# A split-float32 attention layer on one core: a longer distance from scores to transposes and values, four sized probability buffers, and a weight split moved between engines

## The chip, the cores and the metric

One core of a Trainium2 chip runs the whole program. The metric is the device time of one execution in microseconds (us), median over runs. Engines are named as the profile names them: PE (TensorE matmuls and transposes), PEld (its weight loads), DVE (VectorE), ACT (ScalarE), POOL (GpSimd), SP (SyncE, which issues DMAs).

## The reference

One layer with multi-head latent attention in float32: S = 1024 tokens, model width 1024, 16 heads, chunks of 64.

```python
u = h @ w_in
c_q, c_kv, k_rope, z = jnp.split(u, [...])
q = (rmsnorm(c_q, q_norm) @ w_q_b).reshape(B, S, MLA_HEADS, MLA_NOPE + MLA_ROPE)
kv = (rmsnorm(c_kv, kv_norm) @ w_kv_b).reshape(B, S, MLA_HEADS, MLA_NOPE + MLA_V)
...
for blk in range(S // Q_BLOCK):          # query blocks of 128
    s = (q_nope . k_nope + q_rope . k_rope) * scale     # keys 0 .. q1
    s = jnp.where(k_chunk[None, :] <= q_chunk[:, None], s, -jnp.inf)
    prob = jax.nn.softmax(s, axis=-1)
    outs.append(prob @ v[:, :q1])
...
return (o * jax.nn.silu(z)) @ w_out
```

Behind it the layer adds a per-layer embedding, gated by a sigmoid of the residual stream.

## The kernel before

Every float32 product is made of three matmuls in a faster format: each operand is split into a high part (a rounded copy) and a low part (what is left of it, `sub_hi`, L91), and `pairs` runs high by high, high by low, low by high. So a matmul operand always costs a cast (often on ACT) and a subtraction (DVE or GpSimd).

The program has five stages, by time of the profiled execution: the projections of u (0 to 69 us), the z gate and the rotary part of the queries (69 to 188), attention (188 to 520), the output projection (520 to 630), the embedding gate (630 to 741).

In the second stage a loop over eight column blocks `c` (L500 to L528) multiplies h with the z weights (L510); for c from 2 to 5 `project_r` (L421) also multiplies the query latent with a piece of the rotary weights `w_r` (`product_q`, nine matmuls, L417, for each half). Its results are multiplied by cosine and sine on DVE (L429), split into `zT`/`rh` on ACT (L431) and lows on GpSimd, and written to memory by DMAs that GpSimd issues (L434). The rotary weights come through `load_split` (L391): a DMA into one of two staging tiles `ws`, a copy into `wrh` (L397) and a subtraction into `wrl` (L91), both on GpSimd. Each of `wrh` and `wrl` has one buffer. The per-head weights (`wq`, `wk`, `wv`) use the same function.

In attention a step is one pair of a head and a query block i, 128 steps in all. Block i has (i+1)*128 keys. ORDER = (7, 0, 6, 1, 5, 2, 4, 3) alternates large blocks (4 to 7, over 512 keys) with small ones. A step (loop at L690) issues `scores` of its block (L597: matmuls L608, mask L611, row maximum L613 on DVE, exp L618 on ACT with its row sum, which ACT reads out in a second instruction); then the projections that fall due (`project_k` L544, `project_v` L563, `project_q` L585, by the tables K_AT, V_AT, Q_AT of step numbers within a head); then `values` (L659, matmuls L667, output L671 on ACT and L672 on DVE) of a finished half head, LAGV steps later; then `prob_transposes` (L640) of the block LAG steps back: 128x128 transposes on PE (L118), up to four into one tile, a cast to the high part on ACT (L656), a subtraction on DVE (L91). The `p` tiles of halves are `pt0` and `pt1`.

Scores of a large block lie in `ps_big`, of which there are two (a tile of 1024 columns each); all else in attention (`ps_tr`, `ps_pj`, `ps_o`) shares four tiles of 512 columns. A `ps_big` tile is free again when the exp has read it. The exp writes into a probability tile, of which there are three of 1024 columns (`prob_tile`, L541). The framework puts each engine's instructions into a fixed order in advance and adds the waits; the source order and the buffers decide what it may do.

Of the kernel before, what the change touches and what calls it, by code (L numbers as in the profile page):

```python
# [9 lines left out]
F32 = mybir.dt.float32  # L10
# [7 lines left out]
P = 128  # L18
S = 1024
# [4 lines left out]
QL = 384  # L24
# [13 lines left out]
LAST = (7, 0, 6, 1, 5, 2, 3, 4)  # L38
WARM = 9
V_FIRST = (1, 1, 5, 3)  # L40
V_AT, K_AT, Q_AT, ROPE_AT = (5, 5, 3, 3), (1, 3), (7, 5), 4
LAG, LAGV, LEAD, ODD_AT = 2, 4, 2, 1
TWO_PI = 2.0 * math.pi


# [6 lines left out]
def mla_ple_kernel(ctx, tc, x, x_t, p_t, pos, norm_g, w_c, w_z, q_norm, w_q, w_r, kv_norm, w_k, w_v,  # L52
# [7 lines left out]
    V, A, G = nc.vector, nc.scalar, nc.gpsimd  # L60

    def pool(name, bufs=1, **kw):
        return tc.tile_pool(name=name, bufs=bufs, **kw)
# [3 lines left out]
    def ps_big():  # L67
        return psum.tile([P, 1024], F32, tag="big", name="ps_big", bufs=2)

    def ps_tr():  # L70
        return psum.tile([P, 512], F32, tag="one", name="ps_tr", bufs=4)
# [18 lines left out]
    def sub_hi(eng, lo, src, hi):  # L90
        eng.tensor_tensor(out=lo, in0=src, in1=hi.bitcast(F32), op=ALU.subtract)  # L91
# [295 lines left out]
    att1 = late.enter_context(pool("att1", side="right"))  # L387
    att2 = late.enter_context(pool("att2", side="right"))
    k_hi, k_lo = zip(*([att2.tile([P, S], F32R, name=f"k_{z}{e}") for z in ("hi", "lo")] for e in range(2)))

    def load_split(src, cols, name, bufs, home=att1):  # L391
        n = math.prod(cols)
        stg = att1.tile([P, 512], F32, tag="ws", name="ws", bufs=2)[:, :n]
        nc.sync.dma_start(out=stg, in_=src)
        hi = home.tile([P, n], F32R, tag=name + "h", name=name + "h", bufs=bufs)
        lo = home.tile([P, n], F32R, tag=name + "l", name=name + "l", bufs=bufs)
        G.tensor_copy(out=hi, in_=stg)  # L397
        sub_hi(G, lo, stg, hi)
        return tuple(z.rearrange("p (k n) -> p k n", k=cols[0]) for z in (hi, lo))

    wk_of, wv_of, wq_of, q_of, rq_of = {}, {}, {}, {}, {}
# [1 line left out]
    def weights(h):  # L403
        if h >= H:
            return
        if h % 2 == 0:
            wq_of[h // 2] = load_split(w_q[h // 2], (QL // P, P), "wq", 1)
            wk_of[h // 2] = load_split(w_k[h // 2], (KVL // P, P), "wk", 1)
        if h % 4 == 0:
            wv_of[h // 4] = load_split(w_v[h // 4], (KVL // P, 256), "wv", 1)  # L410
# [82 lines left out]
    zw = zph.enter_context(pool("zw", reuse_waits="tile"))  # L493
    cs = [zw.tile([P, S], F32, name=f"cs{e}") for e in range(2)]

    def weights_r(g):
        return load_split(w_r[g], (QL // P, P), "wr", 1, zw)


    for c in range(KT):  # L500
        ps = ps_big()
        for k in range(KT):
            if k % 4 == 0:
                n = 2 * c + k // 4
                wz = wz_of.pop(n)
                if n + 2 < 2 * KT:
                    wz_of[n + 2] = z_weights(n + 2)
            for a, b in pairs:
                for hf in range(2):
                    nc.tensor.matmul(ps[:, hf * 512:(hf + 1) * 512], wz[b][:, k % 4, :],  # L510
                                     (hT_hi, hT_lo)[a][:, k, hf * 512:(hf + 1) * 512],
                                     start=k == 0 and a + b == 0, stop=k == KT - 1 and a == 1)
        V.tensor_tensor(out=zT[:, c, :], in0=ps, in1=rbc, op=ALU.mult)
        A.activation(out=zT[:, c, :], in_=zT[:, c, :], func=AF.Silu)
        if c < 2:
            u_transposes(*pend.pop(0))
        if c == 0:
            rope_tables()
        if c == 1:
            rope_key()  # L520
            wr = weights_r(0)
        if 2 <= c < 6:
            project_r(c - 2, wr, 0, zT[:, 6, :], zT[:, 7, :].bitcast(F32R))
            project_r(c - 2, wr, 1, rt_tile("rt"), rh_tile("rh"))
            if c < 5:
                wr = weights_r(c - 1)
        if c == 6:
            weights(0)  # L528
# [5 lines left out]
    att = atts.enter_context(pool("att"))  # L534
# [3 lines left out]
    vals = att.tile([P, NT, 2, 4, VD], F32R, name="vals")  # L538
    kst = {}

    def prob_tile():  # L541
        return att.tile([P, S], F32, tag="prob", name="prob", bufs=3)

    def project_k(c, hf):  # L544
        w = wk_of[c]
# [48 lines left out]
    def order(h):  # L594
        return LAST if h == H - 1 else ORDER

    def scores(h, i):  # L597
        e = h % 2
        q = q_of[h]
        qs = slice(i * P, (i + 1) * P)  # L600
        n = (i + 1) * P
        off = P if n == 640 else 0
        spans = {128: [(0, 256)], 640: [(0, 384), (384, 640)]}.get(
            n, [(a, min(a + 512, n)) for a in range(0, n, 512)])
        ps = ps_big() if n > 512 else ps_tr()
        for s0, s1 in spans:
            for a, b in pairs:
                nc.tensor.matmul(ps[:, off + s0:off + s1], q[a][:, qs], (k_hi, k_lo)[b][e][:, s0:s1],  # L608
                                 start=a + b == 0, stop=a == 1)
        s = ps[:, off:off + n]  # L610
        V.memset(s[0:64, n - 64:], MASKED)  # L611
        mx = small.tile([P, 1], F32, tag="mx", name="mx")
        V.tensor_reduce(out=mx, in_=s, axis=AX.X, op=ALU.max, negate=True)  # L613
        pr = prob_tile()
        if e == 0 and i == order(h)[0]:
            sums[h // 2] = small.tile([P, 2 * NT], F32, tag="l", name="l", bufs=2)
        l = sums[h // 2][:, e * NT + i:e * NT + i + 1]
        A.activation(out=pr[:, :n], in_=s, func=AF.Exp, bias=mx, scale=1.0, accum_out=l)  # L618
        return pr
# [72 lines left out]
    for n in range(len(blocks) + LAGV):  # L692
        if n < len(blocks):
            h, i = blocks[n]
            at = n % NT
            probs[n] = scores(h, i)
            if h % 2 == 0 and at == ODD_AT:
                odd_k()
            for t in range(NT):
                if h % 4 == 0 and at == (V_AT if h else V_FIRST)[t // 2]:  # L700
                    project_v(h // 4, t)
            if h + 1 < H:
                if h % 2 and at in K_AT:
                    project_k((h + 1) // 2, K_AT.index(at))
                if h % 2 and at == ROPE_AT:
                    rope_q(h + 1)
                    rope_q(h + 2)
                if h % 2 and at in Q_AT:
                    project_q((h + 1) // 2, Q_AT.index(at))
                if h % 2 and at == max(Q_AT):  # L710
                    weights(h + 3)
        h, i = blocks[n - LAGV]
        g = i // 4
        if n >= LAGV and i == [z for z in order(h) if z // 4 == g][-1]:
            values(h, g)
            if h % 2 and i == order(h)[-1] and n < len(blocks):
                normalise(h // 2, lambda hf: att1.tile([P, 512], F32, tag="ws", name="rlb", bufs=2), G)
        if n >= LAG and n - LAG < len(blocks):
            prob_transposes(*blocks[n - LAG], probs.pop(n - LAG))
        if n == len(blocks) - LEAD:  # L720
            og0 = out_part(rh_tile("a0h"), rt_tile("a0l").bitcast(F32R), 0, slice(0, KT - 1), G.tensor_copy)
# [96 lines left out]
    for t in range(NT):  # L818
# [7 lines left out]
        for i, cols in enumerate(spans):  # L826
            n = cols.stop - cols.start
# [74 lines left out]
```

## Time and profile before

| what | value |
|---|---|
| time, median of 3 runs | 740.62 us (740.1 to 742.89) |
| the profiled execution, its own time | 742.71 us |
| its span in the trace | 740.9 us |
| PE busy | 712.6 us, 96% of the span |
| PEld busy | 599.2 us, 81% |
| DVE busy | 525.6 us, 71% |
| ACT busy | 401.2 us, 54% |
| POOL busy | 209.2 us, 28% |

The span is what the trace covers; the execution's own time is 1.8 us longer. PE and PEld overlap: the weights of one matmul load while the one ahead runs. "Busy" counts from the start of an instruction to its modelled end, so that successive matmuls overlap in the rows; the pace of PE is read from one start to the next. PEclk is the granted clock as a share of full speed.

### The profile page before, as it was taken

Reading aid. Unit: us, or ns where it says so; the run is one execution under the profiler, and the core shown is the slowest. Engines: PE = TensorE matmul, PEld = TensorE weight load, DVE = VectorE, ACT = ScalarE, POOL = GpSimd, SP = SyncE. Lnnn points to the kernel's source line nnn. Section 1 sums busy time; section 2 is a strip of 40 time slices with the busy share of each in tenths; the row PEclk is TensorE's granted clock in tenths of the full one; section 3 lists DMA queues with packets and bytes.
Section 4 is the critical chain, followed back from the end, with each engine's and each line's share of the span. In section 5 each row is a group of like instructions: output and inputs, shape, how many; then the busy total and the mean of one; then the engine's idle time right before and its main releaser. Section 6 shows DMA issues by size and latency. Waiting matters only on the chain.

```text
span 740.9 us, 11048 instructions
## 1 busy us (share of the span) xinstructions
PE 712.6 (96%) x3776; PEld 599.2 (81%) x3776; DVE 525.6 (71%) x1270; ACT 401.2 (54%) x921; POOL 209.2 (28%) x204
## 2 busy tenths in 40 slices
PE   8999999979999999999999999999999999999995
PEld 7999888858887778878888788877768887888885
DVE  6995456641887787888788887888555239788854
ACT  6752344331777676777777776776443135243322
POOL 0004316670223232323324232156136132000000
PEclk9999999989999999999999999999999999999998
DMA  8812524462311212101121211033384021110101
GB/s 310 286 56 68 132 77 176 164 216 76 85 44 29 76 30 75 39 27 56 30 75 44 76 29 47 13 115 85 116 297 128 0 86 28 37 43 36 58 28 58
DMA packets 27191, 63.90 MB, mean 86 GB/s; under 512 B 4600, under 2 KB 9088, under 8 KB 27136
## 3 DMA queue, kind: packets, MB, share of 16 engines
q1 hardware_dynamic: 23312, 52.05, 22.6%
q0 software_dynamic: 3536, 11.02, 4.4%
q8 instruction: 30, 0.49, 0.3%
q14 instruction: 25, 0.20, 0.1%
q10 hardware_dynamic: 288, 0.14, 0.1%
HBM read 50.01 MB, written 13.18 MB: 85 GB/s over the span
## 4 chain that ended last, share of the span: by engine, by line
PE 69%; DVE 11%; ACT 8%; issue 4%; DMA 3%; POOL 3%; SPq 0%; ACTq 0%; DVEq 0%; POOLq 0%
PE ps_big L757 17%; PE ps_big L510 9%; PE ps_o L667 9%; PE ps_tr L118 6%; PE ps_big L608 5%; PE ps_pj L417 4%; PE ps_big L212 3%; PE ps_pj L569 3%; PE ps_pj L550 3%; ACT prob L618 3%; DVE pt1l L91 3%; PE ps_pj L757 3%; PE ps_big L213 3%; PE ps_tr L608 2%; DVE mx L613 2%
## 5 line engine op out<-in xcount | busy, mean ns | idle before, releaser
L757 PE MATMUL ps_big<-w,aTh 128*128 128x512 f32 (+1 forms) x480 | 140.2, 392 | 1.8 <-ACT sg L833 1.8
L757 PEld LDWEIGHTS ps_big<-w,aTh 128*128 128x128 f32 x480 | 90.1, 189 | 22.2 <-ACT sg L833 2.2
L118 PE MATMUL ps_tr<-ident,prob 128*128 128x128 f32 x576 | 84.6, 275 | 6.0 <-ACT prob L618 3.3
L757 PE MATMUL ps_big<-w,aTl 128*128 128x512 f32 (+1 forms) x240 | 85.1, 392 | 0.6 <-POOL aTl L91 0.5
L118 PEld LDWEIGHTS ps_tr<-ident,prob 128*128 128x128 f32 x576 | 66.5, 140 | 20.6 <-ACT prob L618 10.2
L674 POOL TENSOR_TENSOR zT<-o,zT 64x512 f32<-64x512 f32 x28 | 36.0, 1287 | 141.2 <-DVE o L672 141.1
L91 DVE TENSOR_TENSOR pt1l<-ps_tr,pt1h 128x512 fp32r<-128x512 f32 (+1 forms) x144 | 72.7, 536 | 3.9 <-ACT pt1h L656 2.5
L656 ACT CAST pt1h<-ps_tr 128x512 fp32r<-128x512 f32 (+1 forms) x144 | 62.0, 470 | 24.2 <-PE ps_tr L118 12.0
L618 ACT ACTIVATE prob<-ps_big,mx 128x1024 f32<-128x1024 f32 (+1 forms) x64 | 61.3, 958 | 18.3 <-DVE mx L613 17.1
L613 DVE TENSOR_REDUCE mx<-ps_big 128x1 f32<-128x1024 f32 (+1 forms) x64 | 64.9, 1015 | 0.3
L358 DVE SCALAR_TENSOR_TENSOR zl<-zs,g_col,zh 128x128 fp32r<-128x128 f32 x56 | 31.3, 607 | 32.9 <-ACT zh L357 32.6
L757 PEld LDWEIGHTS ps_big<-w,aTl 128*128 128x128 f32 x240 | 45.3, 189 | 11.4 <-POOL aTl L91 1.5
L608 PE MATMUL ps_big<-k_hi,qh 128*128 128x512 f32 (+2 forms) x128 | 48.6, 380 | 0.0
L608 PE MATMUL ps_big<-k_hi,ql 128*128 128x512 f32 (+2 forms) x128 | 46.5, 363 | 0.0
L608 PE MATMUL ps_big<-k_lo,qh 128*128 128x512 f32 (+2 forms) x128 | 46.1, 360 | 0.0
L357 ACT ACTIVATE zh<-zs,g_col 128x128 fp32r<-128x128 f32 x56 | 18.3, 392 | 50.2 <-DMA zs<-in_w_z 47.2
L667 PE MATMUL ps_o<-pt1h,vals 128*128 128x512 f32 (+3 forms) x128 | 42.9, 361 | 1.5 <-DVE pt1l L91 1.0
L113 ACT ACTIVATE jk<-xs 128x512 bf16<-128x512 f32 (+2 forms) x25 | 18.7, 750 | 42.3 <-DVE xs L835 35.1
L667 PE MATMUL ps_o<-pt1l,vals 128*128 128x512 f32 (+3 forms) x128 | 41.6, 363 | 0.0
L672 DVE TENSOR_TENSOR o<-ps_o,o 64x512 f32<-64x512 f32 x32 | 22.0, 688 | 25.3 <-ACT o L671 25.2
L618 ACT ACTIVATE prob<-ps_tr,mx 128x128 f32<-128x128 f32 (+1 forms) x64 | 33.8, 529 | 5.5 <-DVE mx L613 5.3
L91 DVE TENSOR_TENSOR pt0l<-ps_tr,pt0h 128x128 fp32r<-128x128 f32 (+2 forms) x80 | 33.2, 416 | 4.5 <-ACT pt0h L656 2.9
(289 smaller groups left out, 1806.7 us busy)
## 6 DMA issues: line engine op xcount, KB each, us to landing
zT<-in_x SPq DMA_DIRECT2D x8, 512.0 KB, 4.5
rlb<-rl SPq DMA_DIRECT2D x32, 128.0 KB, 3.0
wst<-in_w_out SPq DMA_DIRECT2D x8, 512.0 KB, 4.1
xs<-in_x SPq DMA_DIRECT2D x8, 512.0 KB, 7.0
wst<-in_ple_gate SPq DMA_DIRECT2D x8, 512.0 KB, 3.7
zs<-in_w_z SPq DMA_DIRECT2D x14, 256.0 KB, 2.9
out<-xs SPq DMA_DIRECT2D x14, 256.0 KB, 2.0
zT<-in_x_t SPq DMA_DIRECT2D x6, 512.0 KB, 3.7
```

The lines of the kernel that those rows point to most:

```text
L91: eng.tensor_tensor(out=lo, in0=src, in1=hi.bitcast(F32), op=ALU.subtract)
L118: nc.tensor.transpose(dst[:, j * P:(j + 1) * P], src[:, j * P:(j + 1) * P], ident)
L358: V.scalar_tensor_tensor(out=lo[:, k, :], in0=stg[:, k, :], scalar=g, in1=hi[:, k, :].bitcast(F32), op0=ALU.mult, op1=ALU.subtract)
L417: nc.tensor.matmul(ps, w[b][:, k, :], (cq_hi, cq_lo)[a][:, k, hf * 512:hf * 512 + 512], start=k == 0 and a + b == 0, stop=k == n - 1 and a ...
L510: nc.tensor.matmul(ps[:, hf * 512:(hf + 1) * 512], wz[b][:, k % 4, :], (hT_hi, hT_lo)[a][:, k, hf * 512:(hf + 1) * 512], start=k == 0 and ...
L608: nc.tensor.matmul(ps[:, off + s0:off + s1], q[a][:, qs], (k_hi, k_lo)[b][e][:, s0:s1], start=a + b == 0, stop=a == 1)
L613: V.tensor_reduce(out=mx, in_=s, axis=AX.X, op=ALU.max, negate=True)
L618: A.activation(out=pr[:, :n], in_=s, func=AF.Exp, bias=mx, scale=1.0, accum_out=l)
L656: A.copy(out=hi, in_=src[:, ks])
L667: nc.tensor.matmul(ps[:, q * P:], vals[:, j, c % 2, 2 * e:2 * e + 2, :], pt[g][n][:, at:at + 4 - q, :], start=j + n == 0, stop=(j, n) == ( ...
L674: (V if h >= H - 2 else G).tensor_tensor(out=z, in0=o[top], in1=z, op=ALU.mult)
L757: nc.tensor.matmul(o, st[a][:, k, :], w[k][b][:, cols], start=k == 0 and a + b == 0, stop=k == nk - 1 and a == 1)
```

## The change

The attention loop's two distances grow by one step (LAG 2 to 3, LAGV 4 to 5), and the table V_AT, which places the projection of values, moves from steps (5, 5, 3, 3) to (7, 7, 5, 5) of every fourth head. Probabilities get two tiles of 1024 columns and two of 512 in place of three of 1024, which is the same memory; a block takes the smaller kind if it has at most 512 keys. The split of the rotary weights `w_r` is done by ACT (copy) and DVE (subtraction) in place of GpSimd. From L542 on, line numbers are higher by one.

```diff
-V_AT, K_AT, Q_AT, ROPE_AT = (5, 5, 3, 3), (1, 3), (7, 5), 4
-LAG, LAGV, LEAD, ODD_AT = 2, 4, 2, 1
+V_AT, K_AT, Q_AT, ROPE_AT = (7, 7, 5, 5), (1, 3), (7, 5), 4
+LAG, LAGV, LEAD, ODD_AT = 3, 5, 2, 1
...
-    def load_split(src, cols, name, bufs, home=att1):
+    def load_split(src, cols, name, bufs, home=att1, copy=G.tensor_copy, eng=G):
...
-        G.tensor_copy(out=hi, in_=stg)
-        sub_hi(G, lo, stg, hi)
+        copy(out=hi, in_=stg)
+        sub_hi(eng, lo, stg, hi)
...
-        return load_split(w_r[g], (QL // P, P), "wr", 1, zw)
+        return load_split(w_r[g], (QL // P, P), "wr", 1, zw, A.copy, V)
...
-    def prob_tile():
-        return att.tile([P, S], F32, tag="prob", name="prob", bufs=3)
+    def prob_tile(n):
+        n = 512 if n <= 512 else S
+        return att.tile([P, n], F32, tag=f"prob{n}", name="prob", bufs=2)
...
-        pr = prob_tile()
+        pr = prob_tile(n)
```

How the change moves instructions is shown at three places. First the split of the last piece of rotary weights in the second stage. GpSimd's order before:

```order
L397 CAST wrh<-ws 128x384
L397 CAST wvh<-ws 128x512
L91 TENSOR_TENSOR zT<-zT 128x1024
L434 DMA rq2h<-zT 128x2x512
L434 DMA rq2l<-zT 128x2x512
L91 TENSOR_TENSOR rt<-rt,rh 128x1024
L434 DMA rq2h<-rh 128x2x512
L434 DMA rq2l<-rt 128x2x512
L91 TENSOR_TENSOR wrl<-ws,wrh 128x384
L91 TENSOR_TENSOR wvl<-ws,wvh 128x512
```

The same place now, first on ACT, where `wrh` is written:

```order
L514 ACTIVATE zT<-zT 128x1024
L431 CAST zT<-zT 128x1024
L397 CAST wrh<-ws 128x384
L431 CAST rh<-rt 128x1024
L357 ACTIVATE zh<-zs,g_col 128x128 x8
```

and on DVE, where `wrl` is written:

```order
L429 TENSOR_TENSOR zT<-ps_pj,cs_987 128x512
L429 TENSOR_TENSOR zT<-ps_pj,cs_988 128x512
L429 TENSOR_TENSOR rt<-ps_pj,cs_987 128x512
L429 TENSOR_TENSOR rt<-ps_pj,cs_988 128x512
L91 TENSOR_TENSOR wrl<-ws,wrh 128x384
L358 SCALAR_TENSOR_TENSOR zl<-zs,g_col,zh 128x128 x4
```

The subtraction into `wrl` no longer stands behind the two subtractions and four DMA issues of the rotary products; it stands behind the cosine and sine products that DVE makes anyway.

Second, PE in the first steps of an odd head (1, 3 and so on to 13). Names carry the number of the tile: before, `ps_big_3647` holds the scores of block 7, `ps_big_3784` those of block 5, which lie in the same memory. PE before, from the last matmul of block 7:

```order
L608 MATMUL ps_big_3647<-k_hi1_969,ql_3317 128x512
...
L608 MATMUL ps_big_3699<-k_hi1_969,ql_3317 128x384
...
L550 MATMUL ps_pj_3679<-ckv_lo_99,wkh_3418 128x512
L118 MATMUL ps_tr_3690<-ident_61,prob_3639 128x128 x4
L667 MATMUL ps_o_3711<-pt1h_1831,vals_1833 128x512 x2
...
L667 MATMUL ps_o_3711<-pt1l_1832,vals_1833 128x512
L118 MATMUL ps_tr_3732<-ident_61,prob_3657 128x128 x4
L118 MATMUL ps_tr_3739<-ident_61,prob_3657 128x128 x4
...
L608 MATMUL ps_big_3784<-k_hi1_969,qh_3316 128x512
```

and now, where block 7 is `ps_big_3641` and block 5 `ps_big_3767`:

```order
L609 MATMUL ps_big_3641<-k_hi1_969,ql_3300 128x512
L118 MATMUL ps_tr_3653<-ident_61,prob_3588 128x128 x3
L609 MATMUL ps_big_3690<-k_hi1_969,qh_3299 128x512
...
L609 MATMUL ps_tr_3659<-k_hi1_969,ql_3300 128x256
L551 MATMUL ps_pj_3668<-ckv_hi_98,wkh_3406 128x512
...
L551 MATMUL ps_pj_3668<-ckv_lo_99,wkh_3406 128x512
L118 MATMUL ps_tr_3679<-ident_61,prob_3613 128x128 x4
L118 MATMUL ps_tr_3686<-ident_61,prob_3613 128x128
L609 MATMUL ps_big_3767<-k_hi1_969,qh_3299 128x512
```

The sixteen matmuls of `values` (L667) and the transposes behind them no longer lie between the two blocks that share a tile; five transposes do. ACT at that place, before and now:

```order
L618 ACTIVATE prob_3639,l_3445<-ps_tr_3632,mx_3637 128x512
L618 ACTIVATE prob_3657,l_3445<-ps_big_3647,mx_3655 128x1024
L552 CAST k_hi0_967<-ps_pj_3679 64x512
L618 ACTIVATE prob_3677,l_3445<-ps_tr_3670,mx_3675 128x128
L656 CAST pt0h_1829<-ps_tr_3690 128x3x128
```

```order
L657 CAST pt0h_1829<-ps_tr_3653 128x3x128
L619 ACTIVATE prob_3627,l_3439<-ps_tr_3620,mx_3625 128x512
L553 CAST k_hi0_967<-ps_pj_3668 64x512
L619 ACTIVATE prob_3651,l_3439<-ps_big_3641,mx_3649 128x1024
L619 ACTIVATE prob_3666,l_3439<-ps_tr_3659,mx_3664 128x128
```

The exp of block 7 (`prob_3657`, now `prob_3651`) stood ahead of the cast of the key projection and stands behind it now.

Third, the same steps of an even head (head 8). PE before, block 7 in `ps_big_3914`, block 5 in `ps_big_4085`:

```order
L608 MATMUL ps_big_3914<-k_hi0_967,ql_3797 128x512
L417 MATMUL ps_pj_3882<-cq_hi_96,wqh_3412 128x512
...
L417 MATMUL ps_pj_3882<-cq_lo_97,wqh_3412 128x512
L118 MATMUL ps_tr_3908<-ident_61,prob_3828 128x128 x3
L118 MATMUL ps_tr_3927<-ident_61,prob_3859 128x128 x4
L118 MATMUL ps_tr_3934<-ident_61,prob_3859 128x128
L608 MATMUL ps_big_3958<-k_hi0_967,qh_3796 128x512
...
L608 MATMUL ps_tr_3938<-k_hi0_967,ql_3797 128x256
L608 MATMUL ps_big_4085<-k_hi0_967,qh_3796 128x512
```

and now, block 7 in `ps_big_3908`, block 5 in `ps_big_4016`:

```order
L417 MATMUL ps_pj_3870<-cq_lo_97,wqh_3400 128x512
...
L609 MATMUL ps_big_3908<-k_hi0_967,ql_3780 128x512
L118 MATMUL ps_tr_3921<-ident_61,prob_3815 128x128 x3
L609 MATMUL ps_big_3949<-k_hi0_967,qh_3779 128x512
...
L609 MATMUL ps_tr_3927<-k_hi0_967,ql_3780 128x256
L118 MATMUL ps_tr_3938<-ident_61,prob_3854 128x128 x4
L118 MATMUL ps_tr_3945<-ident_61,prob_3854 128x128
L118 MATMUL ps_tr_3961<-ident_61,prob_3868 128x128 x4
L609 MATMUL ps_big_4016<-k_hi0_967,qh_3779 128x512
```

The nine matmuls of the query projection (L417) came between the two blocks and now come ahead of the last matmul of block 7; four more transposes lie between.

## Rows read from the trace of the kernel before

**Rows 1.** Stages: window, length, busy (PE, PEld, DVE, ACT, POOL), PEclk, DMA share, GB/s.

```profile
69.00:188.00 119.00, 114.08 (x500) 93.54 (x498) 62.51 (x116) 43.99 (x94) 51.73 (x58) 0.97 0.44 142
188.00:520.00 332.00, 322.74 (x1923) 272.91 (x1921) 273.87 (x607) 244.67 (x596) 111.21 (x90) 1.00 0.19 52
```

**Rows 2.** Timeline of PE, the second stage's stall: start, duration, instruction, idle time before.

```profile
148.47 0.40 PE L417 MATMUL ps_pj<-cq_hi,wrh 128*128 128x512 f32 x1
153.79 0.80 PE L417 MATMUL ps_pj<-cq_hi,wrl 128*128 128x512 f32 x1 [4.92 <-POOL wrl L91]
...
157.80 0.42 PE L417 MATMUL ps_pj<-cq_hi,wrl 128*128 128x512 f32 x1
```

**Rows 3.** Work in the four microseconds behind that stall.

```profile
154.00:158.00 4.00, 4.00 (x10) 3.14 (x11) 1.56 (x5) 2.22 (x5) 0.96 (x1) 0.52 0.90 340
```

**Rows 4.** Timeline of POOL ahead of the stall's end.

```profile
148.98 2.35 POOL L91 TENSOR_TENSOR rt<-rt,rh 128x1024 fp32r<-128x1024 f32 x1
...
152.73 1.00 POOL L91 TENSOR_TENSOR wrl<-ws,wrh 128x384 fp32r<-128x384 f32 x1
```

**Rows 5.** Timeline of ACT and of DVE some microseconds ahead of the stall.

```profile
140.92 1.28 DVE L429 TENSOR_TENSOR rt<-ps_pj,cs 128x512 f32<-128x512 f32 x2
141.08 1.06 ACT L431 CAST zT<-zT 128x1024 fp32r<-128x1024 f32 x1 [0.71 <-issue]
```

**Rows 6.** PEld's waits in attention: total us, times, longest us.

```profile
PEld ps_tr L118 <- ACT prob L618: 10.2, 19, 1.4
PEld ps_o L667 <- DVE pt1l L91: 3.5, 8, 1.3
PEld ps_tr L608 <- DVE pt0l L91: 2.2, 6, 0.5
PEld ps_tr L608 <- DVE o L672: 1.8, 7, 0.4
```

**Rows 7.** Costly groups by shape: busy us, mean ns of one, idle before.

```profile
L618 ACT ACTIVATE prob<-ps_big,mx 128x1024 f32<-128x1024 f32 x16 | 17.9, 1118 | 2.4 <-DVE mx L613 2.3
L618 ACT ACTIVATION_READ_ACCUMULATOR prob<-ps_big,mx 128x1 f32 x64 | 12.5, 195 | 0.0
L552 ACT CAST k_hi<-ps_pj 64x512 fp32r<-64x512 f32 x16 | 9.2, 577 | 3.0 <-PE ps_pj L550 2.8
L91 DVE TENSOR_TENSOR pt1l<-ps_tr,pt1h 128x384 fp32r<-128x384 f32 x32 | 17.5, 548 | 0.4 <-ACT pt1h L656 0.4
```

**Rows 8.** Timeline of PE: the pace of matmuls of 512 columns and of transposes.

```profile
302.54 0.39 PE L550 MATMUL ps_pj<-ckv_hi,wkl 128*128 128x512 f32 x1
302.77 0.40 PE L550 MATMUL ps_pj<-ckv_lo,wkh 128*128 128x512 f32 x1
...
315.22 1.03 PE L118 MATMUL ps_tr<-ident,prob 128*128 128x128 f32 x8
316.01 0.48 PE L608 MATMUL ps_big<-k_hi,qh 128*128 128x512 f32 x1
```

**Rows 9.** Timeline, an odd head: last score matmul of block 7, then its exp.

```profile
330.71 0.39 PE L608 MATMUL ps_big<-k_hi,ql 128*128 128x512 f32 x1
...
335.06 1.12 ACT L618 ACTIVATE prob<-ps_big,mx 128x1024 f32<-128x1024 f32 x1 [0.24 <-DVE mx L613]
```

**Rows 10.** Timeline, an even head: the same two instructions.

```profile
312.94 0.39 PE L608 MATMUL ps_big<-k_hi,ql 128*128 128x512 f32 x1
...
316.28 1.12 ACT L618 ACTIVATE prob<-ps_big,mx 128x1024 f32<-128x1024 f32 x1
```

**Rows 11.** PE behind a pause at the end of attention and one in the output projection.

```profile
517.13 0.87 PE L118 MATMUL ps_tr<-ident,prob 128*128 128x128 f32 x6 [0.98 <-ACT prob L618]
516.00:520.00 4.00, 3.02 (x18) 2.07 (x17) 3.60 (x10) 3.17 (x9) 0.00 (x0) 1.00 0.00 0
628.23 0.73 PE L757 MATMUL ps_big<-w,aTh 128*128 128x512 f32 x2 [1.80 <-ACT sg L833]
628.50:632.00 3.50, 3.50 (x10) 2.76 (x10) 2.30 (x7) 0.72 (x2) 0.00 (x0) 0.55 0.12 40
```

## The prediction

> **What bounds the kernel now.** I read the work by stage first [rows 1]. PE is busy for 322.74 of 332.00 us in attention and for 114.08 of 119.00 in the stage before it. No other engine comes near: in attention DVE has 273.87 and ACT 244.67. So the time is PE's work, its pauses, and its clock, which shows as 1.00 in attention and 0.97 in the second stage. The second view was PE's timeline where that 0.97 arises: one pause of 4.92 us, released by GpSimd's `wrl` [rows 2], and behind it ten matmuls in 4.00 us at a granted clock of 0.52, which is the 1.2 GHz level [rows 3]. The third was PEld's waits in attention [rows 6], which show pauses that "busy" hides, as a waiting weight load delays its matmul. The largest is the transposes waiting for their exp: 10.2 us in 19 waits, the longest 1.4. The others are many and short. The last was the pace of PE: matmuls of 512 columns start 0.23 us apart (302.54 to 302.77), transposes 0.10, eight from 315.22 to 316.01 [rows 8]. In proportion I take 0.18 for 384 columns and 0.12 for 256, and 0.11 for a transpose, a little over its 0.10 for the change of operands.
>
> **Part 1: the rotary weights off GpSimd.** Before, `wrl` takes 1.00 us but starts only at 152.73, behind a subtraction of 2.35 us that began at 148.98 and two DMA issues [rows 4]. Now it stands behind the second pair of products on DVE, which begins at 140.92 with 1.28 for the pair, and `wrh` behind the cast that begins at 141.08 with 1.06 [rows 5]. The copy is below the 0.577 us that ACT takes for 512 columns on half the partitions; the subtraction costs about 0.548, as DVE takes for the same shape [rows 7]. So `wrh` is there at 141.08 + 1.06 + 0.58 = 142.7 and `wrl` at 143.3. PE asks for it at 148.47 + 0.23 = 148.7 [rows 2], so there are 5 us of slack. The gap from 148.47 to 153.79 is 5.32 and should be 0.23: 5.1 us go. The ten matmuls between 153.79 and 157.80 took 4.01 in place of 2.3: 1.7 go. Together **-6.8 us**. What it adds is four copies and four subtractions, some 0.6 and 0.5 us each, on ACT and DVE, which in this stage are busy for 43.99 and 62.51 of 119 us [rows 1]: nothing, unless the casts behind them come late; were that cover gone, it is the 4.5 us of the eight. GpSimd loses as many. The other pieces' splits caused no pause of their own, so nothing more is gained there.
>
> **Part 2: the longer distance removes waits.** A transpose now follows its exp by one more step, over 1 us of PE work. Nearly all of the 10.2 us on `prob` should go, and I take **-9**; at worst the exps stay as late as PE is early and 5 go, at best 10.2. Values, five steps behind, wait less for `pt1l` (3.5 us): **-3**, between 0 and 3.5. The waits on `pt0l` and `o` for a free small tile (2.2 and 1.8 in [rows 6]) are DVE's backlog; they shrink if PE pauses elsewhere and DVE catches up: **-4**, between 0 and 4. The smaller ones that I don't list I leave as they are. PE's own work stays: each transpose, score and value is issued as before. The four tiles of probabilities hold a block as long as needed: a large block's tile is asked for again four steps later, and its transposes are issued three steps later, so no wait is added there.
>
> **Part 3: the longer distance adds a wait.** The scores of block 5 need the `ps_big` tile of block 7, which is free when ACT has read it for the exp. The order of before has other work between. In an odd head, after block 7's last matmul: twenty transposes, fifteen score matmuls, six of the key projection and sixteen of values. Now the values come after, and five transposes are all that follows the projection. Its cast moved ahead of the exp on ACT. So from the start of the projection's last matmul: 0.39 until it is out (such a matmul's duration in [rows 9]), 0.577 for the cast, 1.118 for the exp, 0.195 for the read-out [rows 7], 2.28 in all. PE has 0.23 for that matmul and 0.55 for five transposes. It then stands for **1.5 us**. A second way: before, from the start of block 7's last matmul to the end of its exp were 335.06 + 1.12 + 0.20 - 330.71 = 5.7 us [rows 9], while PE now has 4.1 us of work there (that matmul 0.23, three transposes 0.33, score matmuls 3 x 0.23, 3 x 0.18 and 3 x 0.12, the projection 1.38, five transposes 0.55): 1.6. In an even head the exp ended 316.28 + 1.12 + 0.20 - 312.94 = 4.7 us after that start [rows 10]; PE had nine matmuls of projection (2.1), eight transposes (0.9), nine score matmuls (1.6) and that matmul itself there, 4.8 us, so it hardly stood; now it has the same without the nine and with twelve transposes, 3.1: 1.6 again. There are seven odd and seven even heads with a block 7 that follows this pattern (heads 1 to 14). At 14 x 1.5, the first way's figure, it is **+21 us**. The lower bound is the exp starting the moment PE has finished the projection, 1.118 + 0.195 + 0.16 - 0.55 = 0.9 or 13 us; the upper is one cast for transposes more ahead of the exp, some 0.4, so 1.9 or 26. DVE and ACT get 21 us of air, which is why I let part 2's backlogs go.
>
> What is queued behind the exp on ACT are casts for transposes; PE stands then too, so they cost nothing twice. The projection of values, moved from steps 5 and 3 to 7 and 5, keeps its work; the tiles it takes are the four small ones. Its waits I put at zero, with the `o` row (1.8) as a bound either way.
>
> **The sum.** -6.8 - 9 - 3 - 4 + 21 = -1.8 us against the profiled execution's 742.71: 740.9. The median shown is 2.1 lower than that execution, so **738.8 us**. With pauses from 13 to 26 and the removed waits from 5 to 17.7, the ends are -11.5 and +14, or 729 and 753.
>
> **The clock.** A pause costs more if the clock falls behind it. The trace has both kinds [rows 11]: behind 0.98 us of PE idle at 517.13 the clock stayed 1.00; behind 1.80 at 628.23 it showed 0.55 for 3.5 us, ten matmuls in 3.5 us that take 2.3 at full pace, so 1.2 us lost, where the second stage lost 1.7 (part 1). A stand of 1.5 us shows as some 1.3 of idle, as the last transpose's pipeline covers 0.17 of it; that is nearer to the former, and PEld's longest wait in attention, 1.4 [rows 6], left the clock at 1.00 [rows 1]. I take no fall. The Trainium skill, "TensorE: Matmul & The Clock Gate", section "A second HAM failure mode: psum-queue depth-cycling", speaks against this change: it describes a kernel whose cycling through PSUM banks left PE idle briefly between groups of matmuls, and whose clock swung between its two levels. By that rule the sum would be that of the second rival below; so far the trace doesn't agree, as attention has waits of up to 1.4 us between groups of matmuls and shows 1.00.
>
> **The rivals.** *Faster*: the pauses come out at the lower bound, 13, and the waits of part 2 go whole, -6.8 - 17.7 + 13 = -11.5: **729 us**. For it: ACT has 87 us free in attention, so the exp may be earlier than its queue suggests. Against: the order on ACT puts the cast ahead of it. *Slower by the clock*: the stand of 1.5 us is long enough to lower it. Where it decides lies between 0.98 and 1.80 of idle; if half the fourteen stands pass it at 1.7 each, 7 x 1.7 = 11.9: **751 us**. For it the row at 628.23, against it the row at 517.13. *Slower without it*: the stands come in full and the waits of part 2 hardly shrink, because DVE's order and not distance sets them; only 5 of the 10.2 go, -6.8 + 21 - 5 = +9.2: **750 us**. For it: DVE is busy for 82% of attention. *The split doesn't gain what it should*: `wrl` is late on DVE behind products that wait for PE, or z lows are late by its 0.5 us. If half of 6.8 stays, **742 us**. Against it: the 5 us of slack.
>
> **How the numbers follow.** A measurement of this kernel tells about 0.5% from no change, 3.7 us, so "same" is 736.9 to 744.3. Forecast 0.60, its own range 731 to 746: 0.27 of it below 736.9, 0.31 within, 0.02 above. Faster rival 0.13. Clock 0.10, waits that stay 0.12, both slower. Split 0.05, within. So faster 0.40, same 0.36, slower 0.24. The range that holds eight in ten goes from 728 to 751: it leaves out the half of the faster rival and of the two slower ones that lie outside.
>
> **What would show it.** The pause of 4.92 and the 0.52 behind it gone, and the second stage at clock 1.00 and 112 us: part 1. PEld's row on `prob` L618 for transposes at 1 to 2 us: part 2. A new row, PE `ps_big` waiting for ACT `prob`, with 14 waits and some 15 to 20 us: part 3. If that row is missing, part 3 is wrong and the time is near 722 (738.8 less 21, and the 4 us that DVE's air was to bring back); if the granted clock in attention is below 1.00, the clock's rival holds.

## The result, and the profile after

The changed kernel takes 750.75 us (median of 4 runs, 749.37 to 750.98) against 740.36 for the kernel before: a ratio of 1.0132, 95% interval 1.0102 to 1.0162. It is slower by 10 us, where 738.8 was forecast. The time lies at the upper end of the stated range (728 to 751), and is clearly slower where about no change was forecast.

The profiled execution took 749.37 us, with a span of 747.5. Its work by stage is below, with the stages' borders as they now lie (the second stage ends at 181.8, attention at 537; columns as in [rows 1]).

```profile
69.00:181.80 112.80, 112.80 (x504) 93.00 (x504) 64.71 (x120) 45.86 (x98) 45.93 (x50) 1.00 0.48 151
181.80:537.00 355.20, 332.08 (x1964) 280.50 (x1962) 279.51 (x615) 245.35 (x603) 110.74 (x90) 1.00 0.18 49
```

The kernel before, cut at the same two events (the first score matmul and the end of the last values):

```profile
69.00:188.30 119.30, 114.38 (x501) 93.77 (x499) 62.81 (x116) 44.29 (x94) 51.73 (x58) 0.97 0.44 142
188.30:526.70 338.40, 329.14 (x1959) 278.35 (x1957) 277.75 (x615) 247.42 (x603) 111.21 (x90) 1.00 0.18 51
```

The second stage is 6.5 us shorter and PE never pauses in it. Attention is 16.8 us longer with the same matmuls: all of the loss is there. What follows attention took 3.7 us less in this pair of executions (210.5 against 214.2), which is about how far the two profiled executions lie to either side of their medians: the pause of 1.80 us in the output projection and the clock's fall behind it [rows 11] don't occur in this one.

**The second stage.** Where PE stood for 4.92 us [rows 2], it now goes on; the split is done 6 us before it is wanted. From the timelines of PE, ACT and DVE:

```profile
148.99 0.40 PE L417 MATMUL ps_pj<-cq_hi,wrh 128*128 128x512 f32 x1
149.22 0.39 PE L417 MATMUL ps_pj<-cq_hi,wrl 128*128 128x512 f32 x1
```

```profile
141.72 0.51 ACT L397 CAST wrh<-ws 128x384 fp32r<-128x384 f32 x1
...
142.27 0.56 DVE L91 TENSOR_TENSOR wrl<-ws,wrh 128x384 fp32r<-128x384 f32 x1 [0.38 <-ACT wrh L397]
```

**PE's waits, whole span**, by their releaser (total, times, longest). The answer to the pause of part 3:

```profile
PE ps_big L609 <- ACT prob L619: 7.7, 9, 1.2
PE ps_tr L118 <- DVE pt0l L91: 6.1, 4, 1.5
PE ps_tr L609 <- DVE ql L91: 3.5, 3, 1.2
```

These are sixteen new stands: seven in the odd heads 1 to 13 and two in head 15 (first row), four in the even heads 2, 4, 8, 12 (second), three in 6, 10, 14 (third). Before, attention's PE waits added up to 6.9 us, none on `ps_big`; now they add up to 21.7.

**PEld's waits in attention**, to be set against [rows 6]:

```profile
PEld ps_big L609 <- ACT prob L619: 12.3, 16, 1.5
PEld ps_tr L118 <- DVE pt0l L91: 7.1, 5, 1.7
PEld ps_tr L609 <- issue: 5.9, 7, 1.5
PEld ps_tr L609 <- ACT row L630: 2.9, 6, 0.5
PEld ps_tr L609 <- DVE pt1l L91: 2.0, 7, 0.6
...
PEld ps_tr L118 <- ACT prob L619: 1.4, 5, 0.4
```

The transposes' wait for their exp fell from 10.2 to 1.4, and the values' wait for `pt1l`, 3.5 before, has no row any more. All rows of this view add up to 30.2 us before and 43.4 now.

**One odd head**, timelines of DVE, ACT and PE. ACT stands for 1.79 us in front of the cast `k_hi`, with the exp of block 7 behind it in its order, whose maximum is ready at 422.99 + 1.20 = 424.19; the exp follows, then PE begins block 5:

```profile
422.99 1.20 DVE L614 TENSOR_REDUCE mx<-ps_big 128x1 f32<-128x1024 f32 x1
424.60 0.58 ACT L553 CAST k_hi<-ps_pj 64x512 fp32r<-64x512 f32 x1 [1.79 <-PE ps_pj L551]
425.08 1.11 ACT L619 ACTIVATE prob<-ps_big,mx 128x1024 f32<-128x1024 f32 x1
```

```profile
424.40 0.71 PE L118 MATMUL ps_tr<-ident,prob 128*128 128x128 f32 x5
426.33 0.50 PE L609 MATMUL ps_big<-k_hi,qh 128*128 128x512 f32 x1 [1.23 <-ACT prob L619]
```

Five transposes from 424.40 take 0.5, so PE stands from about 424.9 to 426.3: 1.4 us. Heads 1, 7 and 11 are like this. The order shown above for all odd heads is not that of the other four: in head 3 two score matmuls stand between the five transposes and block 5, in heads 5, 9 and 13 the six of block 6, and PE idles less. In head 9:

```profile
385.06 0.50 PE L609 MATMUL ps_big<-k_hi,qh 128*128 128x512 f32 x1 [0.48 <-ACT prob L619]
```

**One even head**, timelines of DVE and PE. Here a small tile comes free last: the subtraction into `pt0l`, which frees it, stands behind block 7's maximum on DVE.

```profile
359.43 1.23 DVE L614 TENSOR_REDUCE mx<-ps_big 128x1 f32<-128x1024 f32 x1
360.69 0.56 DVE L91 TENSOR_TENSOR pt0l<-ps_tr,pt0h 128x384 fp32r<-128x384 f32 x1
```

```profile
358.83 0.95 PE L118 MATMUL ps_tr<-ident,prob 128*128 128x128 f32 x5
361.30 0.66 PE L118 MATMUL ps_tr<-ident,prob 128*128 128x128 f32 x4 [1.52 <-DVE pt0l L91]
362.01 0.50 PE L609 MATMUL ps_big<-k_hi,qh 128*128 128x512 f32 x1
```

### The profile page after: what moved, and what is told of

Its sections match the earlier page's. It is cut to its first block, busy times and chain, and to the rows that moved or that the text cites. A ratio compares the mean times of both kernels' runs of the same rounds, so it can differ in the third digit from the quotient of the medians.

```text
span 747.5 us, 10983 instructions
## 1 busy us (share of the span) xinstructions
PE 711.5 (95%) x3776; PEld 598.2 (80%) x3776; DVE 525.5 (70%) x1274; ACT 400.8 (54%) x925; POOL 202.9 (27%) x196
## 4 chain that ended last, share of the span: by engine, by line
PE 76%; ACT 11%; DVE 7%; issue 2%; DMA 2%; POOL 1%; SPq 0%; ACTq 0%; DVEq 0%
PE ps_big L758 21%; PE ps_big L510 12%; PE ps_o L668 8%; PE ps_tr L118 5%; PE ps_pj L417 5%; PE ps_big L609 5%; ACT prob L619 5%; PE ps_big L212 3%; PE ps_tr L609 3%; PE ps_pj L570 3%; PE ps_pj L758 3%; PE ps_pj L551 3%; PE ps_big L213 2%; ACT pt1h L657 2%; DVE mx L614 2%
## 5 line engine op out<-in xcount | busy, mean ns | idle before, releaser
L758 PEld LDWEIGHTS ps_big<-w,aTh 128*128 128x128 f32 x480 | 89.3, 188 | 20.5 <-ACT aTh L687 0.7
L609 PE MATMUL ps_big<-k_hi,qh 128*128 128x512 f32 (+2 forms) x128 | 50.1, 391 | 8.3 <-ACT prob L619 7.7
L358 DVE SCALAR_TENSOR_TENSOR zl<-zs,g_col,zh 128x128 fp32r<-128x128 f32 x56 | 27.9, 546 | 24.2 <-ACT zh L357 23.9
L619 ACT ACTIVATE prob<-ps_tr,mx 128x128 f32<-128x128 f32 (+1 forms) x64 | 34.0, 531 | 10.6 <-DVE mx L614 10.6
```

Source lines behind the costliest of these rows:

```text
L358: V.scalar_tensor_tensor(out=lo[:, k, :], in0=stg[:, k, :], scalar=g, in1=hi[:, k, :].bitcast(F32), op0=ALU.mult, op1=ALU.subtract)
L758: nc.tensor.matmul(o, st[a][:, k, :], w[k][b][:, cols], start=k == 0 and a + b == 0, stop=k == nk - 1 and a == 1)
```

## The experiments

In all, the kernel before ran beside them with a median of 740.3 to 741.0 us. The ratios are to it. Their intervals are 0.3 to 0.6% wide, so two rows that differ by less than some 3 us are not told apart.

The framework makes PE's order, and an edit can move it. Going by the order of PE's 3776 instructions in the traces (buffer numbers left out), the kernel before and e1 have the same, and so have the change and e2. In the other runs some instructions stand elsewhere: at least 45 in e9, 83 in e10 and 136 in e6, against e1; 40 in e5, 45 in e11, 108 in e8 and 114 in e12, against the change. e3, e4 and e7 change the written order itself. So only e1 and e2 show their edit alone; the others show it with what the framework made of it.

| run | median us | ratio (95% interval) |
|---|---|---|
| e1, rotary split alone | 732.34 | 0.9891 (0.9870 to 0.9911) |
| e9, split and tiles | 732.45 | 0.9881 (0.9856 to 0.9906) |
| e10, split, key cast on DVE | 736.49 | 0.9938 (0.9916 to 0.9961) |
| e6, split, shorter exp | 738.62 | 0.9968 (0.9948 to 0.9987) |
| e11, change, shorter maximum and exp | 740.81 | 0.9995 (0.9978 to 1.0011) |
| e8, change, key cast on DVE | 746.84 | 1.0069 (1.0042 to 1.0097) |
| e5, change, shorter exp | 749.22 | 1.0094 (1.0069 to 1.0119) |
| the change | 750.75 | 1.0132 (1.0102 to 1.0162) |
| e7, change, scores last | 750.83 | 1.0118 (1.0089 to 1.0148) |
| e3, change, distances 2 and 5 | 751.08 | 1.0144 (1.0124 to 1.0164) |
| e12, change, old table | 751.47 | 1.0135 (1.0107 to 1.0164) |
| e4, change, distances 3 and 4 | 754.43 | 1.0190 (1.0162 to 1.0217) |
| e2, distance without the split | 757.24 | 1.0223 (1.0201 to 1.0246) |

### The parts apart: e1, e2, e9, e12

e1 is the kernel before with this one edit (and with `load_split` taking the two engines, as in the change):

```diff
-        return load_split(w_r[g], (QL // P, P), "wr", 1, zw)
+        return load_split(w_r[g], (QL // P, P), "wr", 1, zw, A.copy, V)
```

> The kernel before with only the rotary split on ACT and DVE. Theory (the split gains 6.8 us, all of the loss comes from the longer distance): 740.4 - 6.8 = 733.6 us, the second stage without a pause and at clock 1.00, PEld's waits in attention as before, some 30 us. Rival (the split's copies and subtractions are paid for elsewhere, so that part of the 10 us lost is theirs): 738 us or more.

Measured: 732.34, 8 us less than the kernel before beside it (6.6 to 9.6 by the interval). The theory holds, and this is the fastest kernel of the study. Its PEld waits in attention are those of before: its first two rows,

```profile
PEld ps_tr L118 <- ACT prob L618: 10.2, 19, 1.4
PEld ps_o L667 <- DVE pt1l L91: 3.5, 8, 1.3
```

e2 is the changed kernel with that line undone.

> The changed kernel with the rotary split back on GpSimd. Theory (the two parts are independent, the distance alone costs some 17 us): 750.7 + 6.8 = 757.5 us, with the pause of 4.9 us in the second stage back. Rival (they interact): 753 us or less.

Measured: 757.24, 6.5 above the change and 17 above the kernel before. The parts add up to 9 (17 less 8), where the change measured 10.4, within the intervals. PE's order in e1 is that of the kernel before and in e2 that of the change, so the loss comes with the distances, the tiles or the table, and not with the split.

e9 is e1 with the new `prob_tile` (two tiles of each size):

```diff
-LAG, LAGV, LEAD, ODD_AT = 3, 5, 2, 1
+LAG, LAGV, LEAD, ODD_AT = 2, 4, 2, 1
-V_AT, K_AT, Q_AT, ROPE_AT = (7, 7, 5, 5), (1, 3), (7, 5), 4
+V_AT, K_AT, Q_AT, ROPE_AT = (5, 5, 3, 3), (1, 3), (7, 5), 4
```

(against the changed kernel).

> The kernel before with the rotary split and with the two kinds of probability tiles, at the old distances (2 and 4) and the old table for values. Theory (the distance alone costs; the tiles change no wait): 732.3 us within 1, as with the split alone. Rival (two tiles of each kind make the exps wait for a tile): 736 us or more.

Measured: 732.45. The tiles cost nothing. e12 is the changed kernel with the second of these two edits alone.

> The changed kernel with the old table for the projection of values (5, 5, 3, 3). The PE order between blocks that share a large tile is the same. Theory (the table isn't what costs): 750.7 us within 2. Rival (the later projections hold back the values behind them): 746 us or less.

Measured: 751.47, no difference from the change. In it the projection for the next four heads overwrites values that the last head of the four before still needs, so that head's result mixes two groups: with values five steps behind, the table has to move too. The loss belongs to the distance.

### Which distance: e3, e4

```diff
-LAG, LAGV, LEAD, ODD_AT = 3, 5, 2, 1
+LAG, LAGV, LEAD, ODD_AT = 2, 5, 2, 1
```

> The changed kernel with transposes two steps behind again, values still five. In its order every large tile has 4.1 us or more of PE work between the last score matmul of one block and the first of the next in it (2.9 and 3.8 in the changed kernel). Theory (the pauses come from the transposes' distance): no pauses on the large tile, 733.6 - 3.0 for values that no longer wait for pt1l = 730.6 us; the transposes wait for their exp again, some 10 us. Rival (the pauses come from values being late): about 748 us.

Measured: 751.08. Neither theory is tested by it. In the written order, values that come five steps late stand behind the transposes of the next head's first blocks, which then write into the same `pt` tiles: the values of a head are partly made of the next head's probabilities, and they wait for the casts of those. The stands on the large tile shrank to 2.7 us, as the theory had it, but new waits took their place; from PEld's waits in attention:

```profile
PEld ps_tr L118 <- ACT prob L619: 11.8, 19, 1.9
PEld ps_o L668 <- ACT pt0h L657: 8.2, 14, 1.2
PEld ps_o L668 <- DVE pt0l L91: 6.5, 7, 0.9
PEld ps_big L609 <- ACT prob L619: 2.7, 4, 0.7
```

The other way, `LAG` 3 and `LAGV` 4:

> The changed kernel with values four steps behind again, transposes still three. Its order leaves 1.9 to 3.8 us of PE work between two blocks in one large tile, as in the changed kernel. Theory (the transposes' distance): the pauses stay, 750 us, give or take 3. Rival (values being late): 734 us.

Measured: 754.43, and the first row of the same view is `ps_big` on `prob` again, 11.3 us in 15 waits. The stands come with the transposes' distance, at either distance of the values; that e3's kernel has few of them agrees, as far as it can be used.

### What PE stands for: e5, e6, e11

```diff
-        A.activation(out=pr[:, :n], in_=s, func=AF.Exp, bias=mx, scale=1.0, accum_out=l)
+        w = 512 if i == 7 and 0 < h < H - 1 else n
+        A.activation(out=pr[:, :w], in_=s[:, :w], func=AF.Exp, bias=mx, scale=1.0, accum_out=l)
...
-        V.reciprocal(out=rl, in_=l)
+        V.tensor_copy(out=rl, in_=l)
```

> The changed kernel, with the exp of block 7 of heads 1 to 14 made over 512 of its 1024 columns (the rest of the tile keeps old values) and a copy in place of the reciprocal of the row sums. One exp is 0.42 us shorter (1.118 less 0.694). Theory (PE stands in front of block 5 until that exp has read the large tile): 10 of the 14 heads give 0.42 each, the other four, where a small tile comes free last, at most 0.26: 750.7 - 4 to 5 = 746 us. Rival (PE's stand has another cause, ACT only ends about then): 750 us or more.

Measured: 749.22, 1.5 less than the change, between theory and rival and within the noise of either. The profile shows why. The odd head's stand fell as forecast (1.23 to 0.80 us of idle), the even head's did not move at all, and PE got a second, shorter wait just ahead of it:

```profile
337.43 0.50 PE L609 MATMUL ps_big<-k_hi,qh 128*128 128x512 f32 x1 [0.80 <-ACT prob L620]
...
358.48 0.36 PE L609 MATMUL ps_tr<-k_hi,qh 128*128 128x256 f32 x1 [0.75 <-DVE pt1l L91]
361.29 1.12 PE L118 MATMUL ps_tr<-ident,prob 128*128 128x128 f32 x4 [1.51 <-DVE pt0l L91]
```

With that pair of waits the granted clock fell, here and in two more of the four even heads that have it:

```profile
362.00:366.00 4.00, 4.00 (x17) 3.37 (x17) 2.73 (x8) 2.50 (x8) 0.00 (x0) 0.73 0.00 0
```

Each fall costs 1.7 us (0.84 and 0.73 in the two windows from 358 to 366), and the change's profile has one. So attention is as long as there (355.5 against 355.6 us, from the first score matmul to the end of the last values), with 3.4 us more lost to the clock; at an equal clock this profile would be 3.5 us shorter, near the theory. Over all executions the mean granted clock differs by less (0.992 against 0.993). So the odd heads wait for the exp, as part 3 said, and the even heads for DVE. The control, the same edit on e1:

> The same shorter exp (and no reciprocal) in the kernel of before with the rotary split, where block 5 finds its tile free. Theory: no stand to shorten; up to 1 us from transposes that wait for an exp: 731.3 to 732.3 us. Rival (a shorter exp gains anywhere): 728 us.

Measured: 738.62, 6.3 above e1. Neither theory nor rival: a shorter operation made the kernel slower. The framework evidently plans the order with the operations' lengths: with a shorter exp it ordered PE differently; PEld's waits in attention went from 30 to 35 us. A kernel in which the planner reorders is no clean control, and this pair isn't one.

e11 shortens the maximum of block 7 in the same way as the exp (and keeps the reciprocal):

```diff
-        V.tensor_reduce(out=mx, in_=s, axis=AX.X, op=ALU.max, negate=True)
+        w = 512 if i == 7 and 0 < h < H - 1 else n
+        V.tensor_reduce(out=mx, in_=s[:, :w], axis=AX.X, op=ALU.max, negate=True)
...
-        A.activation(out=pr[:, :n], in_=s, func=AF.Exp, bias=mx, scale=1.0, accum_out=l)
+        A.activation(out=pr[:, :w], in_=s[:, :w], func=AF.Exp, bias=mx, scale=1.0, accum_out=l)
```

> The changed kernel with the maximum as well as the exp of block 7 of heads 1 to 14 made over 512 of its 1024 columns (the rest of the probability tile keeps old values): DVE is 0.5 us shorter there, ACT 0.4. Theory (in the even heads the stand ends with DVE, which has that maximum ahead of the subtraction that frees a small tile): the seven even heads' stands of 1.4 to 1.7 us fall by 0.5, so 3.5 us less than with the shorter exp alone (749.2): 745.7 us. Rival (the even heads wait for something else, or the waits come back at another place): 748 us or more.

Measured: 740.81, 8.4 below e5 and 10 below the change. PE's timeline shows the two kinds of even heads:

```profile
315.83 0.36 PE L609 MATMUL ps_tr<-k_hi,qh 128*128 128x256 f32 x1 [0.76 <-DVE ql L91]
...
358.31 0.44 PE L118 MATMUL ps_tr<-ident,prob 128*128 128x128 f32 x2 [0.98 <-DVE pt0l L91]
```

The idle of 1.51 became 0.98, by the 0.5 us that DVE saves. That the gain is larger than 3.5 is mostly the clock: with no idle of 1.5 us left it shows no fall in attention, where e5's profile has three. Attention takes 347.2 us in this profile, 8.3 less than in e5's; 5.1 of it are those falls, and the 3.2 that are left are near the forecast 3.5. The odd heads give a part of them (`ps_big` on `prob` is down to 2.8 us in 3 waits, from 4.5 in 6 in e5). (This profiled execution took 744.87 us, 4 above the median; against e5's profile some 3 us of that stand ahead of and behind attention.)

### Moving the stand: e7, e8, e10

e7 writes the scores of a step behind its values and transposes:

```diff
-            probs[n] = scores(h, i)
...
             prob_transposes(*blocks[n - LAG], probs.pop(n - LAG))
+        if n < len(blocks):
+            probs[n] = scores(*blocks[n])
```

> The changed kernel with the scores of a step written behind the step's values and transposes. By its order the even heads 2 to 14 have over 4.6 us of PE work again between blocks 7 and 5 (1.9 and 2.9 before this edit), the odd ones 3.5 to 4.5 (3.8). Theory (the stands cost what they last): the even heads' 4 x 2.0 + 3 x 1.6 = 12.9 us go, the odd ones' 7 us stay; a few other pairs come closer (3.0 to 4.2 us, block 5 to the next head's block 7) and may give 2 back: 738 to 741 us. Rival (the time is set by ACT and DVE and only shows at these places): 747 us or more.

Measured: 750.83. The even heads' stands on DVE are nearly gone as expected (`pt0l` from 6.1 to 1.0 us, `ql` from 3.5 to 1.7), and the time isn't: the waits came back elsewhere. PEld's largest in attention are now

```profile
PEld ps_tr L118 <- ACT prob L619: 10.0, 17, 1.4
PEld ps_big L609 <- ACT prob L619: 7.2, 8, 1.1
PEld ps_tr L609 <- ACT prob L619: 6.4, 10, 0.9
```

and all of them add up to 43.3, as in the change (43.4). The 10.0 is the very wait that the longer distance was to remove. The rival's time came out; that ACT and DVE set it is one reading, and what the rows show is that the waits move with the order and their sum stays.

e8 takes from ACT the cast that stands ahead of the exp:

```diff
-        A.copy(out=k_hi[0][:NOPE, cols], in_=ps[:NOPE])
+        V.tensor_copy(out=k_hi[0][:NOPE, cols], in_=ps[:NOPE])
```

> The changed kernel with the high part of the key projection cast on DVE, so that no cast that waits for the projection stands ahead of block 7's exp on ACT in the odd heads. Theory: that exp starts 0.9 us earlier; the odd heads' stands (three of 1.4, one of 1.0, three of 0.6) shrink by 0.6 to 0.9 each, 5 us, less what sixteen more casts cost on DVE: 746 us. Rival (DVE, busier, is as late as ACT was): 750 us or more.

Measured: 746.84, 3.9 less than the change; theory. PE's waits in attention:

```profile
PE ps_tr L118 <- DVE pt0l L91: 10.6, 7, 1.5
PE ps_big L609 <- ACT prob L619: 1.6, 4, 0.4
```

The odd heads' 7.7 us are down to 1.6. All seven even heads now stand for `pt0l`, where three stood for `ql` before, and the even heads' rows grew from 9.6 to 10.6 us; this profile has two falls of the clock in attention where the change's has one. So the odd heads gave 6, and the even heads and the clock took some of it back. The same edit on e1:

> The kernel before with the rotary split and the key projection's high part cast on DVE. The same move took 3.9 us off the changed kernel. Theory (it gained there because a cast that waits stood ahead of block 7's exp): here that exp is ahead of the cast, so 732.3 us within 1.5. Rival (any load off ACT gains, at either distance): 728.5 us.

Measured: 736.49, 4.1 slower than e1, so not the rival, and worse than the theory. PE's transposes now wait for the subtraction `k_lo`, which on DVE stands behind the moved cast (0.2 us in e1):

```profile
PE ps_tr L118 <- DVE k_lo L91: 3.2, 6, 0.6
```

So the edit gains 3.9 where the cast holds back an exp that PE waits for, and loses 4.1 where it doesn't. How much of either the framework's new order makes is not shown: in e10 more of PE's instructions moved (83) than in e9, which kept its time.

## Why the prediction was wrong, step by step

**Part 1, right.** -6.8 us forecast; the second stage is 6.5 shorter, and the split alone gives 8.0 with an interval that includes 6.8. `wrl` was ready at 142.27 + 0.56 = 142.8, forecast 143.3.

**Part 3, right in size, half right in cause, and near the sum by luck.** +21 forecast for fourteen stands of 1.5. The sixteen rows' 17.3 us of idle are 0.2 each short of the stand (1.4 against 1.23 above), so 20.5, and seven even heads stand 0.27 again at the large tile: 22.4. In the odd heads the chain was the forecast one, cast, exp, tile (e5, e8), and in heads 1, 7 and 11, which have the order that the forecast was worked out from, the stand is 1.4. I took that order for all odd heads; the other four have more work there, and the seven come to 7.4 in place of 10.5. In the even heads another release is the last: DVE's, behind the maximum of block 7 (e11). I had looked only at the tile that two blocks share, and took the small tiles' waits for a term of their own; these seven come to 12.9 in place of 10.5. The other 2.1 are in head 15, which I had left out.

**Part 2, the step that failed.** It took 16 us off ("-9", "-3" and "-4"), left the smaller waits as they are, and put those of the projection of values at zero. The four rows that it names did go: 17.7 us before, 1.4 now (10.2 to 1.4, and no row any more for the other three). What failed is what it left at nothing. Of the 43.4 us of PEld's waits now, 23.4 belong to the stands (the 12.3 on the large tile, 6.8 of the 7.1 after `pt0l`, and 4.3 of the 5.9 shown as "issue", which are heads 6, 10 and 14). Without them and the 1.4, 18.6 are left, where the rows that part 2 doesn't name had 12.5: waits of 6.1 us more took the place of the old ones. Among them are block scores that wait for a small tile after `row` (2.9) or `pt1l` (2.0), query projections that wait after `o` (1.6), and shorter ones. So attention's 16.8 us are -16.3 + 6.1 + 23.4 in this view and 1.7 for a fall of the clock (below); 1.9 stand in no row, and their cause stays open. The forecast had -16 + 21. I credited the waits without asking what PE would wait for next.

e7 says it more plainly: when the even heads' stands were ordered away, the transposes waited for their exps again, and the sum of the view stayed at 43. "DVE and ACT get 21 us of air" was half the picture: they did get idle time, but in their fixed order they spent much of it in front of an instruction whose operand PE had not made yet, as ACT does for 1.79 us at 424.60. ACT's waits for PE's values and key projection, from 190 to 505 us, before and now:

```profile
ACT o L671 <- PE ps_o L667: 9.3, 21, 0.9
ACT k_hi L552 <- PE ps_pj L550: 2.8, 8, 0.4
ACT o L672 <- PE ps_o L668: 18.3, 14, 2.2
ACT k_hi L553 <- PE ps_pj L551: 14.1, 11, 1.8
```

**The clock, nearly right, and a rival at its edge.** No fall was taken. The two rows that spoke for it are one event: PEld's wait of 1.4 us in [rows 6] is the one at 517.13, where PE itself idled 0.98 [rows 11], so nothing between 0.98 and 1.80 of idle had been seen. The stands with 1.23 us of idle or less left the clock at 1.00. Of the four with 1.52, one was followed by a fall in this profile; in e2, whose PE order is the same, two of the four were. Both cases of the change's profile, from PE's timeline, the same work behind them:

```profile
271.04 0.66 PE L118 MATMUL ps_tr<-ident,prob 128*128 128x128 f32 x4 [1.52 <-DVE pt0l L91]
...
276.91 0.23 PE L668 MATMUL ps_o<-pt1h,vals 128*128 128x128 f32 x1
...
365.57 0.23 PE L668 MATMUL ps_o<-pt1h,vals 128*128 128x128 f32 x1
```

From 271.04 to 276.91 are 5.87 us; from 361.30 to 365.57, after the same idle, 4.27. The difference is 1.6 us, as priced (1.7). The profiled execution has the highest mean clock of the change's four (0.995; the others 0.992 or 0.993), which for the others is some 2 us more lost, about one fall more. The Trainium skill, "TensorE: Matmul & The Clock Gate", section "A second HAM failure mode: psum-queue depth-cycling", has the clock swing when PE idles between groups of matmuls: the trace agrees behind one stand of sixteen, and not behind the other fifteen.

**The chances.** Slower had 0.24. The clock's rival gave 751, but the falls account for 2 to 4 us of the loss and not for 12. The rival that came nearest in its sum is "slower without it", 750 us, at 0.12; its reason (the waits of part 2 hardly shrink) is not what the rows show: the named waits went, and others came. So its number is luck too. The upper end is also mis-added: 740.6 + 14 is 754.6, not 753.

What stays open, beside the 1.9 us: whether any order would make a distance of three pay. e7 and e8 are two others, both slower than e1 by 14 us or more, but the framework makes the order and I changed only what it is given.

## What to carry to other kernels

A wait that is removed from an engine near its limit is worth its length only if the next release is earlier too: before crediting it, name what that engine would then wait for, and when that is ready, from rows. Where engines run in a fixed order, look for what stands ahead of the critical operation on its own engine and waits itself; moving that one cast came with a gain of 3.9 us here, and with a loss of 4.1 us in the kernel where it held back nothing. An edit that changes a length can also change the planned order, so compare the orders before calling a run a control. And split a change before judging it: one line of this one is worth 8 us (732.3), and the rest cost 18.

## What the runs showed of the hardware that was not expected

PE idle of 1.5 us was followed by a fall of the clock at times and not at others: of four such stands in one execution, with the same work ahead and behind, one was followed by a granted clock of 0.78 over four microseconds, and three were not; 1.23 and less left it at 1.00. In e5, where 0.75 of idle came shortly ahead of 1.51 in four heads, the clock fell in three of them, to 0.73 in the window shown there. In e7 several shorter waits close together (0.41, 0.74 and 0.18 between 315.8 and 318.2) were followed by 0.57. Windows of the changed kernel behind two of the four stands:

```profile
270.00:274.00 4.00, 2.91 (x12) 2.35 (x13) 3.90 (x11) 2.42 (x7) 0.00 (x0) 0.78 0.00 0
364.00:368.00 4.00, 4.00 (x28) 3.65 (x27) 1.88 (x6) 3.10 (x7) 0.27 (x1) 1.00 0.00 0
```

And DVE's subtractions into `zl` in the second stage took 1.23 us for four at 138.27, but 2.87 for two at 144.92, while GpSimd ran a subtraction of its own (145.20, 2.45 us). It is no single case: of the 112 in the traces before and after, the 16 that overlap a subtraction on GpSimd took 0.47 to 3.44 us, the other 96, some of them beside GpSimd's casts and DMA issues, 0.34 to 0.36. From the timelines of DVE and POOL:

```profile
138.27 1.23 DVE L358 SCALAR_TENSOR_TENSOR zl<-zs,g_col,zh 128x128 fp32r<-128x128 f32 x4 [2.96 <-ACT zh L357]
...
144.92 2.87 DVE L358 SCALAR_TENSOR_TENSOR zl<-zs,g_col,zh 128x128 fp32r<-128x128 f32 x2 [2.09 <-ACT zh L357]
145.20 2.45 POOL L91 TENSOR_TENSOR zT<-zT 128x1024 fp32r<-128x1024 f32 x1
```

No pause of PE was traced to it. The change took four of GpSimd's subtractions away there, and the cases fell from eleven to five.
